# State space branch of a hybrid encoder: all products and sums on VectorE, in more and smaller steps, with earlier loads

## Chip, cores and metric

The kernel runs on one core of a Trainium2 chip. The metric is the device time of one execution in microseconds (us), median of several runs. PE is TensorE, DVE is VectorE, ACT is ScalarE, POOL is GpSimd, and SP is SyncE, whose queue issues most DMAs.

## What is computed

One layer of a trunk over 1024 positions of width 1024, in fp32: a norm, one input projection, three branches (a 2-D Fourier mix, a neighbourhood attention of 8 heads, a bidirectional state space scan), gates, an output projection, and a feed-forward part. The branch that the change touches is, cut down:

```python
def _ssm_scan(ug, a_re, a_im, log_dt, b_re, b_im, c_re, c_im, reverse):
    lam_bar = exp(lam * dt)                                # complex, 16 groups x 64 states
    b_bar = ((lam_bar - 1) / lam) * b
    bu = einsum('bsgc,gpc->bsgp', ug, b_bar)
    xs = associative_scan(x[s] = lam_bar * x[s-1] + bu[s]) # along the 1024 positions
    return real(einsum('bsgp,gcp->bsgc', xs, c))

y = d_skip * u + scan(forward) + scan(reverse)
y = gelu(y);  y = y * sigmoid(y @ w_glu)
```

## The kernel before

Every fp32 matrix is split into a high and a low part, and a product is three matmuls of 128x512 (L171, L165). Weights come through a queue (`w_next`, `w_cut`): a DMA, a cast on ACT (L142), a subtraction on DVE (L143). The program is written as one main stream on PE, in the order of a list of steps: the projection of the scan's input, eight tiles of v, then logits of the gates, the q and k projections of four pairs of heads, the gates and the rest. Two generators run beside it. `mm_main` calls `tick` after every third matmul; the state space branch (`ssm`) goes on by 0.4 steps at each tick, the attention by 0.57, where one step is the code up to the next `yield`. A scheduler then orders each engine's instructions by this program order and the buffers that are free; SBUF buffers come from pools (`m`: 21 buffers, `s`: 36), and PSUM has 8 banks (`ps`).

The state space branch works on four quarters q of 4 groups each. `ssm_params` computes the small coefficients, on POOL for the most part, among them `bbar` (POOL) and `bhat` (DVE). `ssm_prep` (generator `matrices`) makes for each quarter two matrices AA and BB by complex products (`product`, tiles of 128x512), the padded `bz`, the transposes BT of BB (PE L464, evicted by ACT L465), and a matrix M by way of `kp` (PE L469, ACT L473 to L475, DVE L477 and L478, eight small DMAs). `ssm_data` multiplies the input U with BT on PE, turns the result by E (L505 to L511), runs four scans (L515, L517), turns back (L523 to L530), and on PE multiplies with M and AA into Y, which is stored to `y_scr`. `ssm_gelu` loads two quarters as `yT` (L552) and applies the gelu on ACT and DVE (L555 to L561); at the end of `ssm` the weights `w_glu` are loaded, and the gate is computed (L597 to L626) and spilled to DRAM (`b_scr`), from where the gate step `u0` loads it as `act`.

In a complex product POOL and DVE share the six instructions of 128x512: POOL makes the two products L430 and L434 and the sum L437, DVE L431, L432 and L435. In `ssm_data` POOL makes `rz` (L495), two sums (L507, L511), two products and a sum of the turn back (L523, L527, L530).

Of the kernel before, what the change touches and what calls it, by code (L numbers as in the profile page):

```python
# [10 lines left out]
F32 = mybir.dt.float32  # L11
# [53 lines left out]
class Trunk:  # L65
# [354 lines left out]
    def ssm_prep(self, q):  # L420

        nc, V, G, A = self.nc, self.nc.vector, self.nc.gpsimd, self.nc.scalar
        g0 = 4 * q
        gs = slice(g0, g0 + 4)
        pa, bbar, bhat = self.ssm_pa, self.ssm_bb, self.ssm_bh

        def product(out, x, y, sh):

            t, u = self.m(sh, F32, "pt"), self.m(sh, F32, "pt")
            G.tensor_tensor(out=t, in0=x[1], in1=y[1], op=ALU.mult)  # L430
            V.tensor_tensor(out=out[:, 0], in0=x[0], in1=y[0], op=ALU.mult)  # L431
            V.tensor_tensor(out=u, in0=x[1], in1=y[0], op=ALU.mult)  # L432
            yield
            G.tensor_tensor(out=out[:, 1], in0=x[0], in1=y[-1], op=ALU.mult)  # L434
            V.tensor_tensor(out=out[:, 0], in0=out[:, 0], in1=t, op=ALU.subtract)  # L435
            yield
            G.tensor_tensor(out=out[:, 1], in0=out[:, 1], in1=u, op=ALU.subtract if len(y) == 3 else ALU.add)  # L437
            yield

        U = self.m([P, 4, NK], F32, "U")  # L440
        self.dma(U, self.u_scr[64 * q:64 * q + 64].rearrange("(g c) (s k) -> (c s) g k", g=4, k=NK))
        AA = self.s([P, 2, 4, 8, 16], F32, "AA")
        sh = [P, 4, 8, 16]
        yield from product(AA, [self.ssm_cc[:, i, gs, :].unsqueeze(2).to_broadcast(sh) for i in range(2)],
                           [pa[:, i, gs, :].unsqueeze(3).to_broadcast(sh) for i in range(3)], sh)
        BB = self.s([P, 2, 4, 16, 8], F32, "BB")
        sh = [P, 4, 16, 8]
        yield from product(BB, [bhat[:, i, gs, :].unsqueeze(3).to_broadcast(sh) for i in range(2)],
                           [pa[:, i, gs, ::-1].unsqueeze(2).to_broadcast(sh) for i in range(2)], sh)
        AA = AA.rearrange("p i g s c -> p i g (s c)")  # L450
        bz = self.m([P, 2, 4, 64], F32, "bz")
        G.memset(bz, 0.0)
        for i in range(2):
            G.tensor_copy(bz[0:64, i, :, 0:16], bbar[0:64, i, gs, :])
            G.tensor_copy(bz[64:128, i, :, 32:48], bbar[64:128, i, gs, :])
        yield
        for _ in range(5 if q == 0 else 0):
            yield
        BT = self.s([P, 4, 2, P], F32, "BT")
        for b in range(2):  # L460
            ps = self.ps([P, 2, 2, P])
            for j in range(2):
                for i in range(2):
                    nc.tensor.transpose(ps[:, j, i, :], BB[:, i, 2 * b + j].rearrange("p c s -> p (c s)"), self.ident)  # L464
            A.copy(BT[:, 2 * b:2 * b + 2], ps)  # L465
            yield
        ps = self.ps([64, 4, P])
        for j in range(4):
            self.mm(ps[:, j, :], [(bz[:, i, j, :], AA[:, i, j, :]) for i in range(2)])  # L469
        kp = self.s([16, 4, 15, 16], F32, "kp")  # L470
        psv = ps.rearrange("p g (s c) -> p g s c", s=8)
        kt = self.m([16, 4, 16], F32, "kt")
        A.copy(kp[:, :, 7:15, :], psv[0:16])  # L473
        A.copy(kp[:, :, 0:7, :], psv[32:48, :, 0:7, :])
        A.copy(kt, psv[32:48, :, 7, :])  # L475
        yield
        V.tensor_tensor(out=kt, in0=kt, in1=self.ssm_dd[:, gs, :], op=ALU.add)  # L477
        V.tensor_tensor(out=kp[:, :, 7, :], in0=kp[:, :, 7, :], in1=kt, op=ALU.add)  # L478
        yield
        M = self.m([P, 4, P], F32, "M")  # L480
        for s in range(8):
            self.dma(M[s::8], kp[:, :, 7 - s:15 - s, :].rearrange("p g t c -> p g (t c)"))
        yield
        self.ssm_mat[q] = (AA, BT, M, U)

    def ssm_data(self, q):
# [5 lines left out]
        L = 4 * NK  # L492
        flat = lambda t: t.rearrange("p g k -> p (g k)")
        rz = self.m(sh, F32, "rz")
        G.tensor_tensor(out=rz, in0=self.ssm_keep[:, 0, 4 * q:4 * q + 4].unsqueeze(2).to_broadcast(sh),  # L495
                        in1=self.kmask.unsqueeze(1).to_broadcast(sh), op=ALU.mult)
        pv = []
        for i in range(2):
# [5 lines left out]
        ta, tb, tc_, td = (self.m(sh, F32, "v") for _ in range(4))  # L504
        V.tensor_tensor(out=ta, in0=pv[0], in1=E[:, 0], op=ALU.mult)  # L505
        V.tensor_tensor(out=tb, in0=pv[1], in1=E[:, 1], op=ALU.mult)
        G.tensor_tensor(out=ta, in0=ta, in1=tb, op=ALU.add)  # L507
        yield
        V.tensor_tensor(out=tc_, in0=pv[1], in1=E[:, 0], op=ALU.mult)
        V.tensor_tensor(out=td, in0=pv[0], in1=E[:, 1], op=ALU.mult)  # L510
        G.tensor_tensor(out=tc_, in0=tc_, in1=td, op=ALU.subtract)  # L511
        yield
        zs = [self.m(sh, F32, "z") for _ in range(2)]
        for v, z in ((ta, zs[0]), (tc_, zs[1])):
            V.tensor_tensor_scan(out=flat(z)[0:64, 1:L], data0=flat(rz)[0:64, 0:L - 1], data1=flat(v)[0:64, 0:L - 1],  # L515
                                 initial=0.0, op0=ALU.mult, op1=ALU.add)
            V.tensor_tensor_scan(out=flat(z)[64:128, 0:L - 1][:, ::-1], data0=flat(rz)[64:128, 1:L][:, ::-1],  # L517
                                 data1=flat(v)[64:128, 1:L][:, ::-1], initial=0.0, op0=ALU.mult, op1=ALU.add)
            V.memset(z[0:64, :, 0], 0.0)
            V.memset(z[64:128, :, NK - 1], 0.0)  # L520
            yield
        ta, tb, tc_, td = (self.m(sh, F32, "v") for _ in range(4))
        G.tensor_tensor(out=ta, in0=zs[0], in1=E[:, 0], op=ALU.mult)  # L523
        V.tensor_tensor(out=tb, in0=zs[1], in1=E[:, 1], op=ALU.mult)
        V.tensor_tensor(out=td, in0=zs[1], in1=E[:, 0], op=ALU.mult)
        yield
        G.tensor_tensor(out=tc_, in0=zs[0], in1=E[:, 1], op=ALU.mult)  # L527
        V.tensor_tensor(out=ta, in0=ta, in1=tb, op=ALU.subtract)
        yield
        G.tensor_tensor(out=tc_, in0=tc_, in1=td, op=ALU.add)  # L530
        yield
        yield
        ps = self.ps(sh)
# [11 lines left out]
    def ssm_gelu(self, hf):  # L545
# [4 lines left out]
        for _ in range(3):  # L550
            yield
        self.tc.keep_in_program_order(self.dma(yT, self.y_scr[8 * hf:8 * hf + 8].rearrange("g c s k -> (g c) s k")))  # L552
        t1, g2 = self.s([P, 8, NK], F32, "t1"), self.s([P, 8, NK], F32, "g2")
        yield
        A.activation(t1, yT, AF.Square)  # L555
# [9 lines left out]
    def ssm(self):  # L565
# [9 lines left out]
        def data():  # L575
            for q in range(4):
                while q not in self.ssm_mat:
                    yield
                yield from self.ssm_data(q)

        def after():
            for hf in range(2):
                while self.y_done < 2 * hf + 2:
                    yield
                yield from self.ssm_gelu(hf)

        self.y_done = 0
# [1025 lines left out]
```

## Time and profile before

| | us |
|---|---|
| median of 3 runs | 1432.58 |
| lowest, highest | 1430.61, 1438.53 |
| the profiled execution | 1433.98 |
| its span | 1432.2 |
| PE busy in the span | 1383.5 |
| DVE, ACT, POOL busy | 947.0, 572.0, 188.8 |

Time zero is the start of the span. In a timeline a row has start, duration, engine, line, operation, tiles, shapes, and in brackets how long the engine idled before it and what ended that. In the table of stretches a row has the stretch, its length, the busy time of each engine with its instructions, the granted clock of PE as a share of 2.4 GHz (0.50 is the lower level, 1.2 GHz), the share of the DMA engines and GB/s. Matmuls overlap in the pipeline: a matmul of 128x512 lasts 0.39 us in a row, but rows follow each other every 0.227 us. On DVE rows overlap too, a little.

### The profile page before, as it was taken

Reading aid. Unit: us, or ns where it says so; the run is one execution under the profiler, and the core shown is the slowest. Engines: PE = TensorE matmul, PEld = TensorE weight load, DVE = VectorE, ACT = ScalarE, POOL = GpSimd, SP = SyncE. Lnnn points to the kernel's source line nnn. Section 1 sums busy time; section 2 is a strip of 40 time slices with the busy share of each in tenths; the row PEclk is TensorE's granted clock in tenths of the full one; section 3 lists DMA queues with packets and bytes.
Section 4 is the critical chain, followed back from the end, with each engine's and each line's share of the span. In section 5 each row is a group of like instructions: output and inputs, shape, how many; then the busy total and the mean of one; then the engine's idle time right before and its main releaser. Section 6 shows DMA issues by size and latency. Waiting matters only on the chain.

```text
span 1432.2 us, 18648 instructions
## 1 busy us (share of the span) xinstructions
PE 1383.5 (97%) x6520; PEld 1152.1 (80%) x6520; DVE 947.0 (66%) x1764; ACT 572.0 (40%) x1087; POOL 188.8 (13%) x313
## 2 busy tenths in 40 slices
PE   6999988999999999999999999999999999999997
PEld 5778877788888888888788878888888788888885
DVE  6759876576473312543524797777777999878766
ACT  5512264566562211032401674333323364444244
POOL 3758611000000000000000003112211100000000
PEclk9999999999999999999999999999999999999998
DMA  6332453737563217411343226444447885454303
GB/s 227 136 121 82 132 165 99 215 111 239 170 215 127 99 42 255 145 43 35 96 162 114 78 89 213 140 154 148 143 155 265 278 298 176 147 175 143 96 8 117
DMA packets 110926, 209.62 MB, mean 146 GB/s; under 512 B 13681, under 2 KB 46833, under 8 KB 110833
## 3 DMA queue, kind: packets, MB, share of 16 engines
q1 hardware_dynamic: 100160, 174.09, 37.6%
q0 software_dynamic: 10672, 34.35, 6.5%
q8 instruction: 51, 0.84, 0.2%
q14 instruction: 43, 0.34, 0.1%
HBM read 146.52 MB, written 56.62 MB: 142 GB/s over the span
## 4 chain that ended last, share of the span: by engine, by line
PE 83%; DVE 7%; DMA 2%; issue 2%; ACT 1%; POOL 1%; SPq 1%; DVEq 0%; ACTq 0%; POOLq 0%
PE ps L165 45%; PE ps L171 34%; PE ps L789 1%; PE ps L806 1%; PE ps L810 1%; SPq L111 1%; DVE z L515 1%; DVE z L517 1%; DVE wl L143 0%; DMA vj<-v_scr 0%; PE ps L1083 0%; DMA bm<-in_rpb 0%; DVE BB L431 0%; DMA wr<-in_w_in 0%; DVE sm L764 0%
## 5 line engine op out<-in xcount | busy, mean ns | idle before, releaser
L165 PE MATMUL ps<-dw,dh 128*128 128x512 f32 x1344 | 306.1, 389 | 2.3 <-DVE dw L197 2.3
L165 PE MATMUL ps<-fb,uw 128*128 128x512 f32 x1344 | 306.6, 389 | 1.4 <-DVE t L1142 1.0
L165 PEld LDWEIGHTS ps<-dw,dh 128*128 128x128 f32 x1344 | 252.0, 188 | 55.7 <-DVE dw L197 3.2
L165 PEld LDWEIGHTS ps<-fb,uw 128*128 128x128 f32 x1344 | 251.9, 188 | 54.5 <-PE ps L1083 1.2
L171 PE MATMUL ps<-hTh,wh 128*128 128x512 f32 x576 | 231.7, 403 | 6.3 <-DVE mx L764 2.0
L171 PE MATMUL ps<-hTl,wh 128*128 128x512 f32 x576 | 227.6, 395 | 1.1 <-DVE hTl L200 1.1
L171 PE MATMUL ps<-hTh,wl 128*128 128x512 f32 x576 | 226.9, 394 | 0.0
L171 PEld LDWEIGHTS ps<-hTh,wh 128*128 128x128 f32 x576 | 109.3, 190 | 28.0 <-ACT wh L142 2.4
L171 PEld LDWEIGHTS ps<-hTh,wl 128*128 128x128 f32 x576 | 109.0, 189 | 22.9
L171 PEld LDWEIGHTS ps<-hTl,wh 128*128 128x128 f32 x576 | 109.5, 190 | 21.2 <-DVE hTl L200 1.5
L143 DVE TENSOR_TENSOR wl<-wr,wh 128x1024 fp32r<-128x1024 f32 (+2 forms) x76 | 72.5, 966 | 55.3 <-ACT wh L142 52.3
L196 ACT CAST dh<-da 128x512 fp32r<-128x512 f32 x112 | 69.5, 620 | 95.4 <-PE ps L165 61.2
L1379 DVE TENSOR_TENSOR x<-x,ps 128x512 f32<-128x512 f32 x112 | 73.6, 684 | 34.4 <-PE ps L165 34.3
L1295 POOL DMA_DIRECT2D h_scr<-hx x48 | 26.0, 541 | 493.7 <-ACT hx L1265 376.1
L197 DVE TENSOR_TENSOR dh<-da,dh 128x512 fp32r<-128x512 f32 x112 | 77.1, 688 | 13.8 <-ACT dh L196 13.8
L171 PE MATMUL ps<-act,wh 128*128 128x512 f32 x256 | 78.7, 390 | 0.1
L142 ACT CAST wh<-wr 128x1024 fp32r<-128x1024 f32 (+2 forms) x76 | 60.7, 821 | 32.1 <-PE ps L171 7.7
L196 ACT CAST uw<-us 128x512 fp32r<-128x512 f32 x64 | 38.1, 626 | 84.2 <-DVE us L1222 84.2
L1017 ACT ACTIVATE tg<-ps 128x512 f32<-128x512 f32 x32 | 19.1, 597 | 124.0 <-PE ps L171 118.6
L1267 DVE SCALAR_TENSOR_TENSOR hx<-hx 128x512 f32<-128x512 f32 x52 | 35.8, 689 | 40.7 <-ACT hx L1259 40.3
L764 DVE CUSTOM_DVE_ANT_0 sm<-ps,bm 128x384 f32<-128x384 f32 x64 | 35.3, 553 | 34.2 <-PE ps L165 24.2
L196 ACT CAST dw<-wd 128x512 fp32r<-128x512 f32 x80 | 49.4, 618 | 19.1 <-PE ps L165 18.4
(286 smaller groups left out, 2116.6 us busy)
## 6 DMA issues: line engine op xcount, KB each, us to landing
da<-h_scr SPq DMA_DIRECT2D x112, 256.0 KB
wr<-in_w_in SPq DMA_DIRECT2D x36, 512.0 KB
wu<-in_w_up SPq DMA_DIRECT2D x32, 512.0 KB
h_scr<-hs POOLq DMA_DIRECT2D x64, 256.0 KB, 2.6
wd<-in_w_down SPq DMA_DIRECT2D x64, 256.0 KB
bm<-in_rpb SPq DMA_DIRECT2D x64, 192.0 KB
h_scr<-hx POOLq DMA_DIRECT2D x48, 256.0 KB, 2.8
vj<-v_scr SPq DMA_DIRECT2D x128, 64.0 KB
```

Of the source, the lines that this page charges most:

```text
L111: return self.nc.sync.dma_start(out=out, in_=in_)
L142: self.nc.scalar.copy(hi, r)
L143: self.nc.vector.tensor_tensor(out=lo, in0=r, in1=hi.bitcast(F32), op=ALU.subtract)
L165: self.nc.tensor.matmul(out=out, lhsT=l, rhs=r, start=start and i == 0, stop=stop and i == last, skip_group_check=more)
L171: self.nc.tensor.matmul(out=out, lhsT=l, rhs=r, start=i == 0, stop=i == last)
L196: nc.scalar.copy(hi, src)
L197: nc.vector.tensor_tensor(out=lo, in0=src, in1=hi.bitcast(F32), op=ALU.subtract)
L764: V.tensor_tensor_reduce(out=sm, in0=ps[:, 0:384], in1=bm.pop(u), scale=-1.0, scalar=3.0e38, op0=ALU.add, op1=ALU.min, accum_out=mx)
L1017: A.activation(tg, ps, AF.Tanh, scale=0.5)
L1267: V.scalar_tensor_tensor(out=x, in0=x, scalar=0.0, in1=x, op0=ALU.max, op1=ALU.mult)
L1295: self.nc.gpsimd.dma_start(out=self.t.h_scr[c, j - 1], in_=x)
L1379: self.nc.vector.tensor_tensor(out=self.x1[t][:, cs], in0=self.x1[t][:, cs], in1=self.banks[j][q], op=ALU.add)
```

## The change

DVE does what POOL did in the products and in `ssm_data`; ACT does POOL's copies into `bz` (only its memset stays on POOL). `product` uses one temporary instead of two, and the turn back writes into the tiles of the turn before. There are more `yield`s: one more in the turn, two more in the scans, one more for the first quarter before BT, and six more between the load of `yT` and its use. The load of `w_glu` stands ahead of the second half's gelu.

```diff
         def product(out, x, y, sh):
-            t, u = self.m(sh, F32, "pt"), self.m(sh, F32, "pt")
-            G.tensor_tensor(out=t, in0=x[1], in1=y[1], op=ALU.mult)
+            t = self.m(sh, F32, "pt")
+            V.tensor_tensor(out=t, in0=x[1], in1=y[1], op=ALU.mult)
             V.tensor_tensor(out=out[:, 0], in0=x[0], in1=y[0], op=ALU.mult)
-            V.tensor_tensor(out=u, in0=x[1], in1=y[0], op=ALU.mult)
             yield
-            G.tensor_tensor(out=out[:, 1], in0=x[0], in1=y[-1], op=ALU.mult)
             V.tensor_tensor(out=out[:, 0], in0=out[:, 0], in1=t, op=ALU.subtract)
+            V.tensor_tensor(out=t, in0=x[1], in1=y[0], op=ALU.mult)
             yield
-            G.tensor_tensor(out=out[:, 1], in0=out[:, 1], in1=u, op=ALU.subtract if len(y) == 3 else ALU.add)
+            V.tensor_tensor(out=out[:, 1], in0=x[0], in1=y[-1], op=ALU.mult)
+            V.tensor_tensor(out=out[:, 1], in0=out[:, 1], in1=t, op=ALU.subtract if len(y) == 3 else ALU.add)
             yield
...
         for i in range(2):
-            G.tensor_copy(bz[0:64, i, :, 0:16], bbar[0:64, i, gs, :])
-            G.tensor_copy(bz[64:128, i, :, 32:48], bbar[64:128, i, gs, :])
-        yield
-        for _ in range(5 if q == 0 else 0):
+            A.copy(bz[0:64, i, :, 0:16], bbar[0:64, i, gs, :])
+            A.copy(bz[64:128, i, :, 32:48], bbar[64:128, i, gs, :])
+        yield
+        for _ in range(6 if q == 0 else 0):
             yield
...
-        G.tensor_tensor(out=rz, ...)
+        V.tensor_tensor(out=rz, ...)
...
         V.tensor_tensor(out=tb, in0=pv[1], in1=E[:, 1], op=ALU.mult)
-        G.tensor_tensor(out=ta, in0=ta, in1=tb, op=ALU.add)
         yield
         V.tensor_tensor(out=tc_, in0=pv[1], in1=E[:, 0], op=ALU.mult)
         V.tensor_tensor(out=td, in0=pv[0], in1=E[:, 1], op=ALU.mult)
-        G.tensor_tensor(out=tc_, in0=tc_, in1=td, op=ALU.subtract)
+        yield
+        V.tensor_tensor(out=ta, in0=ta, in1=tb, op=ALU.add)
+        V.tensor_tensor(out=tc_, in0=tc_, in1=td, op=ALU.subtract)
         yield
...
+            V.memset(z[0:64, :, 0], 0.0)
+            yield
             V.tensor_tensor_scan(out=flat(z)[64:128, 0:L - 1][:, ::-1], ...)
-            V.memset(z[0:64, :, 0], 0.0)
             V.memset(z[64:128, :, NK - 1], 0.0)
             yield
-        ta, tb, tc_, td = (self.m(sh, F32, "v") for _ in range(4))
-        G.tensor_tensor(out=ta, in0=zs[0], in1=E[:, 0], op=ALU.mult)
+        V.tensor_tensor(out=ta, in0=zs[0], in1=E[:, 0], op=ALU.mult)
         V.tensor_tensor(out=tb, in0=zs[1], in1=E[:, 1], op=ALU.mult)
+        yield
         V.tensor_tensor(out=td, in0=zs[1], in1=E[:, 0], op=ALU.mult)
-        yield
-        G.tensor_tensor(out=tc_, in0=zs[0], in1=E[:, 1], op=ALU.mult)
+        V.tensor_tensor(out=tc_, in0=zs[0], in1=E[:, 1], op=ALU.mult)
+        yield
         V.tensor_tensor(out=ta, in0=ta, in1=tb, op=ALU.subtract)
-        yield
-        G.tensor_tensor(out=tc_, in0=tc_, in1=td, op=ALU.add)
+        V.tensor_tensor(out=tc_, in0=tc_, in1=td, op=ALU.add)
         yield
...
         self.tc.keep_in_program_order(self.dma(yT, ...))      # ssm_gelu
+        for _ in range(6):
+            yield
...
                 while self.y_done < 2 * hf + 2:               # ssm, after()
                     yield
+                if hf == 1:
+                    glw.append(self.m([P, 2, 2, P], F32, "glw"))
+                    self.dma(glw[0], self.a["w_glu"])
                 yield from self.ssm_gelu(hf)
...
-        wr = self.m([P, 2, 2, P], F32, "glw")
-        self.dma(wr, self.a["w_glu"])
-        self.split(wh, wl, wr)
+        self.split(wh, wl, glw.pop())
```

The scheduler gives every engine another order of instructions from the first quarter's matrices on; from the fourth pair of heads to the end the orders are the same. Line numbers of the changed kernel lie up to 6 above those of before. Numbers behind a tile's name tell its instances apart.

DVE at the first quarter's matrices, before, from the first product of BB to its real part (vt is the low part of a tile of v, bhat the coefficients of which BB is made, pt the temporaries):

```order
L431 TENSOR_TENSOR BB_819<-bhat_751,pa_746 128x512
L244 TENSOR_TENSOR bhat_751<-tb_759 128x256
L435 TENSOR_TENSOR AA_784<-AA_784,pt_785 128x512
L197 TENSOR_TENSOR vt_811<-ps_775,vt_811 128x8x64
L432 TENSOR_TENSOR pt_821<-bhat_751,pa_746 128x512
L435 TENSOR_TENSOR BB_819<-BB_819,pt_820 128x512
```

DVE at the same place, now:

```order
L431 TENSOR_TENSOR BB_818<-bhat_751,pa_746 128x512
L436 TENSOR_TENSOR BB_818<-bhat_751,pa_746 128x512
L433 TENSOR_TENSOR AA_784<-AA_784,pt_785 128x512
L197 TENSOR_TENSOR vt_810<-ps_775,vt_810 128x8x64
L244 TENSOR_TENSOR bhat_751<-tb_759 128x256
L434 TENSOR_TENSOR pt_785<-ssc_507,pa_746 128x512
L430 TENSOR_TENSOR pt_819<-bhat_751,pa_746 128x512
L437 TENSOR_TENSOR AA_784<-AA_784,pt_785 128x512
L433 TENSOR_TENSOR BB_818<-BB_818,pt_819 128x512
L197 TENSOR_TENSOR vt_847<-ps_814,vt_847 128x8x64
L434 TENSOR_TENSOR pt_819<-bhat_751,pa_746 128x512
L437 TENSOR_TENSOR BB_818<-BB_818,pt_819 128x512
```

From AA's first product to BB's last sum DVE now has 20 instructions, 14 of 512 and 6 of 256 columns, where it had 13, 7 and 6; PE has six more matmuls of the main stream ahead of the first transposes of BB.

ACT at the start of the first pair of heads, before (t is the gelu's tile, BT the transposes of the last quarter's BB, kp a part of its M, sm the scores, tg a gate's logits):

```order
L1042 ACTIVATE tg_1642<-ps_1572 128x512
L555 ACTIVATE t_287_1620<-yT_1535 128x1024
L465 COPY BT_1659<-ps_1660 128x512
L465 COPY BT_1659<-ps_1675 128x512
L559 ACTIVATE t_287_1620<-t_287_1620 128x1024
L473 COPY kp_1701<-ps_1692 16x4x128
```

ACT at the same place, now:

```order
L465 COPY BT_1612<-ps_1613 128x512
L142 CAST wh_1673<-wr_1504 128x1024
L465 COPY BT_1612<-ps_1633 128x512
L777 ACTIVATE sm_1643,su_1646<-sm_1643,mx_1644 128x384
L1048 ACTIVATE tg_1668<-ps_1574 128x512
L777 ACTIVATE sm_1656,su_1659<-sm_1656,mx_1657 128x384
```

The gelu of the first half (L555, now L558) stands 47 instructions behind the second eviction of BT, at the end of this pair; in SP's queue the load of `yT` for it stands right behind the eight DMAs of the last quarter's M, which start from `kp`.

DVE between the first and the second pair of heads, before (OT is the attention's output, spl its low part; L764 reads the second pair's first scores):

```order
L819 TENSOR_TENSOR OT_1584<-ps_2361,ot_2396 64x16x16
L819 TENSOR_TENSOR OT_1584<-ps_2373,ot_2409 64x16x16
L197 TENSOR_TENSOR spl_2424<-OT_1584,sph_2423 128x1024
L143 TENSOR_TENSOR wl_2475<-wr_2341,wh_2474 128x1024
L764 ISA sm_2512,mx_2513<-ps_2509,bm_2444 128x384
```

DVE at the same place, now, up to the scans (L505 and L506 stand just ahead):

```order
L825 TENSOR_TENSOR OT_1523<-ps_2299,ot_2331 64x16x16
L825 TENSOR_TENSOR OT_1523<-ps_2311,ot_2346 64x16x16
L511 TENSOR_TENSOR v_2340<-v_2340,v_2341 128x512
L508 TENSOR_TENSOR v_2342<-ps_2323,E_638 128x512
L509 TENSOR_TENSOR v_2343<-ps_2294,E_638 128x512
L197 TENSOR_TENSOR spl_2362<-OT_1523,sph_2361 128x1024
L512 TENSOR_TENSOR v_2342<-v_2342,v_2343 128x512
L143 TENSOR_TENSOR wl_2419<-wr_2275,wh_2418 128x1024
L516 SCALAR_TENSOR_TENSOR z_2398<-rz_2292,v_2340 64x511
L520 SCALAR_TENSOR_TENSOR z_2398<-rz_2292,v_2340 64x511
L516 SCALAR_TENSOR_TENSOR z_2399<-rz_2292,v_2342 64x511
L520 SCALAR_TENSOR_TENSOR z_2399<-rz_2292,v_2342 64x511
```

The last quarter's data steps (20 instructions on DVE, four of them scans, ten behind the rows shown) now stand here, ahead of the second pair's first scores (now L770). Before they stood among the first pair's scores, where the third quarter's now stand. From the first pair's first scores to the second pair's DVE has 18 more instructions of 128x512, four more scans and four more small memsets than before. The 24 matmuls of the gate (L597 to L626) with their work on ACT and DVE have moved from the second pair of heads to the third.

## Rows read from the trace of the kernel before

**Rows 1.** The page's part 1: busy time, share of the span, instructions.

```profile
PE 1383.5 (97%) x6520; PEld 1152.1 (80%) x6520; DVE 947.0 (66%) x1764; ACT 572.0 (40%) x1087; POOL 188.8 (13%) x313
```

**Rows 2.** Stretches: length, busy PE, PEld, DVE, ACT, POOL, clock, DMA, GB/s.

```profile
79.90:83.10 3.20, 0.39 (x3) 0.20 (x2) 3.16 (x4) 0.00 (x0) 3.20 (x5) 0.88 0.40 164
83.10:89.20 6.10, 6.10 (x18) 5.02 (x19) 0.69 (x1) 1.66 (x3) 2.47 (x6) 0.50 0.64 258
89.20:174.70 85.50, 85.17 (x459) 70.96 (x457) 70.40 (x83) 21.68 (x36) 61.28 (x49) 1.00 0.35 100
174.70:242.00 67.30, 55.94 (x321) 47.82 (x321) 47.59 (x110) 36.82 (x82) 9.18 (x7) 0.95 0.46 132
242.00:255.70 13.70, 13.70 (x62) 11.33 (x61) 3.29 (x4) 4.40 (x7) 0.00 (x0) 1.00 0.67 222
255.70:324.00 68.30, 63.95 (x329) 53.49 (x328) 47.16 (x104) 43.81 (x91) 0.00 (x0) 0.98 0.54 162
324.00:410.00 86.00, 86.00 (x464) 74.03 (x463) 51.95 (x145) 52.23 (x121) 0.00 (x0) 1.00 0.66 195
```

**Rows 3.** PE's timeline, single rows from 79 to 277 us.

```profile
79.31 0.39 PE L171 MATMUL ps<-wl,hTh 128*128 128x512 f32 x1
79.54 0.39 PE L171 MATMUL ps<-wh,hTl 128*128 128x512 f32 x1
...
82.01 0.30 PE L464 MATMUL ps<-konst,BB 128*128 128x128 f32 x1 [2.08 <-DVE BB L435]
...
181.58 0.49 PE L165 MATMUL ps<-U,M 128*128 128x128 f32 x2 [1.96 <-ACT BT L465]
...
188.90 0.52 PE L789 MATMUL ps<-konst,sm 128*128 128x128 f32 x3 [2.23 <-DVE sm L781]
...
276.54 0.62 PE L789 MATMUL ps<-konst,sm 128*128 128x128 f32 x3 [2.31 <-ACT sm L779]
```

**Rows 4.** DVE's timeline, the first quarter's matrices.

```profile
69.63 0.68 DVE L431 TENSOR_TENSOR AA<-ssc,pa 128x512 f32<-128x512 f32 x1
...
78.22 0.41 DVE L244 TENSOR_TENSOR bhat<-tb 128x256 f32<-128x256 f32 x1
78.56 0.68 DVE L435 TENSOR_TENSOR AA<-AA,pt 128x512 f32<-128x512 f32 x1
79.16 0.68 DVE L197 TENSOR_TENSOR vt<-ps,vt 128x512 fp32r<-128x512 f32 x1
```

**Rows 5.** POOL's timeline, a step of the coefficients.

```profile
63.13 0.65 POOL L240 TENSOR_TENSOR tb<-ssb,pt 128x256 f32<-128x256 f32 x1
```

**Rows 6.** DVE by form, 40 to 340 us: busy, mean ns, idle before.

```profile
L517 DVE TENSOR_TENSOR_SCAN z<-rz,v 64x511 f32<-64x511 f32 x8 | 12.5, 1564 | 0.2
...
L431 DVE TENSOR_TENSOR BB<-bhat,pa 128x512 f32<-128x512 f32 x4 | 5.6, 1401 | 0.0
...
L623 DVE SCALAR_TENSOR_TENSOR y<-tg,g 128x512 f32<-128x512 f32 x4 | 4.6, 1159 | 0.1
```

**Rows 7.** DVE's timeline: a scan beside busy POOL, and one without it.

```profile
136.58 2.13 DVE L517 TENSOR_TENSOR_SCAN z<-rz,v 64x511 f32<-64x511 f32 x1
...
217.72 1.22 DVE L517 TENSOR_TENSOR_SCAN z<-rz,v 64x511 f32<-64x511 f32 x1
```

**Rows 8.** ACT's timeline: both halves' gelu, with the idle time before.

```profile
180.00 1.06 ACT L555 ACTIVATE t<-yT 128x1024 f32<-128x1024 f32 x1 [12.08 <-DMA wr<-in_w_in]
...
259.68 1.06 ACT L555 ACTIVATE t<-yT 128x1024 f32<-128x1024 f32 x1 [3.28 <-DMA yT<-y_scr]
```

**Rows 9.** SP's timeline: when the first half's load is issued.

```profile
174.49 0.43 SPq L111 DMA_DIRECT2D yT<-y_scr  x1
```

**Rows 10.** Waits of DVE, 174.7 to 255.7 us: total, times, longest.

```profile
DVE OT L819 <- ACT ot L818: 7.3, 2, 7.1
DVE t L557 <- ACT t L555: 5.7, 1, 5.7
```

**Rows 11.** Issues of the loads of b_scr: ns, first and last start.

```profile
L111 SPq DMA_DIRECT2D act<-b_scr x24: 319/380/679, 414.7 to 579.4; - x24
```

More of the change, by code (lines that the diff above doesn't have):

```diff
@@ L494, in ssm_data @@
         rz = self.m(sh, F32, "rz")
-        G.tensor_tensor(out=rz, in0=self.ssm_keep[:, 0, 4 * q:4 * q + 4].unsqueeze(2).to_broadcast(sh),
+        V.tensor_tensor(out=rz, in0=self.ssm_keep[:, 0, 4 * q:4 * q + 4].unsqueeze(2).to_broadcast(sh),
                         in1=self.kmask.unsqueeze(1).to_broadcast(sh), op=ALU.mult)
@@ L579, in data @@
                 yield from self.ssm_data(q)
+        glw = []
         def after():
```

## The prediction

> **What bounds the kernel now.** I read the page's busy times first, then the table of stretches, then the waits of the engine that bounds. PE is busy for 1383.5 of the span's 1432.2 us [rows 1]: it is the bound nearly everywhere, so the change can only pay where PE idles or runs at the lower clock, and only lose where it makes PE wait. The stretches show where the state space branch makes PE do either [rows 2]. From 89.20 to 174.70 us PE has no gap (85.17 of 85.50), although DVE is busy for 70.4 and POOL for 61.3 there. Three places lose time. The first is the first quarter's matrices: 79.90 to 83.10 has 0.39 us of PE, and the 6.10 us behind it run at half the clock. The second is the first pair of heads (174.70 to 255.70, two rows, 81.0 us): 67.30 − 55.94 = 11.36 us idle and a clock of 0.95. The third is the second pair: 68.30 − 63.95 = 4.35 us idle and 0.98. The third pair (324.00 to 410.00) loses nothing. What ended the idle times [rows 3]: a part of BB from DVE (2.08 us), BT from ACT (1.96), sm from DVE (2.23) and from ACT (2.31).
>
> **First quarter's matrices.** PE now loses 3.20 − 0.39 = 2.81 us idle, and 6.10 us at half clock give back 3.05 us less work [rows 2]: 5.86 us. In the changed kernel DVE makes everything alone: 14 instructions of 512 and 6 of 256 columns from AA's first product, which started at 69.63. In a row they follow each other at 0.60 us (78.56 to 79.16) and 0.34 us (78.22 to 78.56) [rows 4]; so BB is ready at 69.63 + 14 × 0.60 + 6 × 0.34 + 0.2 for the last one's end = 80.3. Before, it was ready only at about 82.0, since DVE's instructions beside POOL were long: the products L431 of BB lasted 1.40 us on average [rows 6]. PE would reach the transposes at 82.01 − 2.08 = 79.93, and has six more matmuls of the main stream ahead of them, at 0.227 us each (79.31 to 79.54 in the rows, rounded) [rows 3]: 81.3. The unknown is POOL: its last four coefficient instructions (L241 to L244), now scattered among products, come right behind L240, four at 0.65 us [rows 5], 2.6 us in which DVE's small steps ahead of 69.63 may stretch. I take 1.5 us of that, the middle and a little: BB at 81.8, 0.5 to 0.7 us of idle time, and no half clock, since the half clock came behind a gap of 2.8. **Gain 5.2 us.** Bounds: 5.9 (no gap at all), and 1.1 (the whole 2.6, so 1.7 idle, and the half clock stays).
>
> The rows show what running beside POOL costs: the same scan took 2.13 us at 136.58, while POOL worked, and 1.22 us at 217.72 without it [rows 7]. The Trainium skill gives a reason ("SBUF — State Buffer", Who interferes with whom): DVE and GpSimd share a port pair as an exclusive lock, so the one that loses waits for the other's whole instruction. By that rule the whole 2.6 us would be lost, and this gain would lie between 1.1 and 4.2 us. The trace agrees that something is shared, but a stretch from 1.22 to 2.13 is less than POOL's time, so I keep the middle.
>
> **From 89.20 to 174.70.** DVE gets 28 products of 128x512 more there and gives four with a PSUM input and four scans to later: 24 × 0.60 − 4 × 1.22 [rows 4, 7] = +9.5 us on 70.4, 79.9 of 85.5 [rows 2], even if no instruction becomes shorter now that POOL is idle; and some will, as the scans do (mean 1.56 against 1.22 us [rows 6, 7]). I cost it at nothing; PE's matmuls cover it. If that cover is thin at one place, up to 2 us.
>
> **First pair of heads.** ACT waited 12.08 us for `yT` ahead of its gelu at 180.00 [rows 8], since the load was issued at 174.49 only [rows 9]. Behind the gelu on ACT stood both evictions of BT; so PE waited 1.96 us for BT, and later 2.23 for sm, which DVE had begun late, having waited 5.7 us for the gelu itself [rows 3, 10]. Now BT's evictions stand 47 instructions ahead of the gelu: these 4.2 us go. Against it stands DVE. It was busy for 47.59 + 3.29 = 50.9 us of the 81.0 [rows 2], and gets 18 × 0.60 + 4 × 1.22 = 15.7 more: 66.6. PE without idle time and clock loss needs 81.0 − 11.36 − 0.05 × 67.3 = 66.2. The two are level, so what counts is how much of DVE's 30.1 us of waits stays. Three blocks should go: 5.7 for the gelu, 7.1 for `ot` [rows 10], since DVE is no longer ahead of PE there, and the 13.70 − 3.29 = 10.4 at the end [rows 2], where the last quarter's data steps now stand. With those gone 6.9 us stay: 73.5. From PE's side, if all but the 4.2 stays, 76.8. I take 75, between them: **gain 6.0 us**. Bounds: 14.8 (66.2, no loss left) and a loss of 2.9 (the last block finds no free time: 66.6 + 17.3 = 83.9).
>
> What is late next is the second pair's start: the last quarter's 20 instructions (12 × 0.60 + 4 × 1.22 = 12.1 us) come on top of 3.29 in 13.70 us, 1.7 too many; a late DVE holds PE at the first sm. I take half, 0.8.
>
> **Second and third pair.** In the second, the gate leaves. ACT's wait of 3.28 us for the second `yT` at 259.68 [rows 8] and PE's 2.31 us at 276.54 [rows 3] with the clock loss behind it, 0.02 × 68.3 = 1.4 [rows 2], go: −2.3 − 1.4 + 0.8 = **gain 2.9 us**. Bounds: 5.8 (4.35 + 1.4, no loss left) and a loss of 1.7 (the stalls stay, DVE is late in full). The third pair gets the gate and the gelu's second half: four instructions of 1.16 us (L623) [rows 6] and two of 1.2 or so on DVE, 7 us on 51.95 of 86.0 [rows 2]. There is room, but the gate's chain through ACT and DVE made gaps where it stood. **Loss 1.2 us**, half of 2.31; bounds nothing and 3.7 (2.3 + 1.4). The gate's later stores must land ahead of the loads of `b_scr`, the first issued at 414.7 [rows 11]; the gate stands inside the third pair, which ends at 410.0, so this costs nothing. From the fourth pair on nothing changes.
>
> **Sum**, against the profiled execution's 1433.98 us: −5.2 − 6.0 − 2.9 + 1.2 = −12.9, so 1421 us. That execution lies 1.4 above the median of 1432.58 and inside the runs' spread (1430.61 to 1438.53); I don't take the 1.4 off.
>
> **Rivals.** (1) *Nothing is left over:* with free engines the three places lose nothing: −5.9 − 14.8 − 5.8 = −26.5, 1407.5 us. For it: PE's third pair runs so today with DVE at 60%. Against: DVE's 66.6 in the first pair would have to fit without a gap. (2) *A wait is replaced by a wait:* POOL's bunched steps stretch DVE's chain, the first BB is late as before (−1.1), and in the first pair PE waits for DVE's sm as long as it did for BT (0); −1.1 − 2.9 + 1.2 = −2.8, 1431 us. For it: the two engines are level there. (3) *DVE becomes the bound of the first pair, and the program slower:* if DVE keeps its 30.1 us of waits, which the attention's chain through PE, ACT and DVE causes and not the work's amount, the stage lasts 66.6 + 30.1 = 96.7, +15.7; with the first gain kept and nothing from the second pair, −5.2 + 15.7 + 1.2 = +11.7, 1445.7 us. It decides from 81.0 − 66.6 + 5.2 − 1.2 = 18.4 us of DVE waits in that stage. Against it: over 20 of the 30.1 lie where DVE had run out of work. The Trainium skill speaks for this rival ("Perfetto Trace Analysis", Optimizing Scalar/DVE Operations): if DVE is saturated, it advises giving work away, to GPSIMD too, while it warns that moves between these two may not help because they share a port. The change goes the other way; the trace agrees with the warning at the scans, and says of saturation only that DVE is near it in this one stage.
>
> **Chances.** The forecast (1414 to 1427) 0.57, rival 1 0.10, rival 2 0.24, rival 3 0.09. Within 0.5% (7.2 us, about what a measurement of this kernel can tell from no change) means 1425.4 to 1439.7. Faster: rival 1 and nearly all of the forecast's, 0.62; the same: its upper end, rival 2 and the lower part of rival 3, 0.31; slower: 0.07. The range of 8 in 10: down to 1410, where most of rival 1 is left out, and up to 1434, which takes in rival 2 and leaves out rival 3.
>
> **What will show it.** First BB: PE's row of the first L464 transposes should have a wait under 1 us, and the stretch behind it clock 1.00; a wait of 2 says that POOL's steps stretched the chain. First pair: no wait of ACT for `yT` ahead of BT, DVE busy for 64 to 67 us in 73 to 77; if DVE is under 80% busy and the stage is longer than 81, rival 3 holds. Second pair: PE idle under 3 us. Third: PE idle of 1 us or so. Scans at 1.22 us throughout. The prediction falls if PE gets a gap between 89 and 174 us, which I cost at nothing, or if one of the first pair's gaps drops PE to half clock for long.

## The result, and the profile after

The changed kernel took 1418.05 us (median of 4 runs, 1417.74 to 1419.28) against 1432.65 of the kernel before in the same comparison: a ratio of 0.9893, 95% interval 0.9864 to 0.9923, so 14.6 us or 1.1% less. Forecast were 1421 us and a gain of 12.9. The profiled execution took 1417.89 us, its span 1416.1.

Part 1 of the page of the changed kernel:

```profile
PE 1378.0 (97%) x6520; PEld 1150.0 (81%) x6520; DVE 952.3 (67%) x1812; ACT 577.3 (41%) x1103; POOL 109.2 (8%) x249
```

Against [rows 1] PE idles 38.1 us instead of 48.7 and is busy for 5.5 us less with as many matmuls; 2.8 us of that, summed over stretches of 2 us, are less time lost at the lower clock. DVE, with 48 instructions more, is busy for only 5.3 us more.

Stretches of the changed kernel (columns as in [rows 2]): the way to the first transposes of BB, what follows, the way to the first scores, the first, the second and the third pair of heads:

```profile
63.73:83.00 19.27, 19.27 (x86) 15.94 (x86) 19.05 (x53) 5.86 (x13) 4.87 (x8) 1.00 0.29 108
83.00:95.00 12.00, 12.00 (x65) 9.82 (x64) 3.45 (x7) 2.96 (x6) 0.00 (x0) 1.00 0.42 162
95.00:168.34 73.34, 73.34 (x393) 61.32 (x392) 61.62 (x96) 24.51 (x46) 1.05 (x2) 1.00 0.37 108
168.34:242.02 73.68, 68.29 (x374) 58.74 (x373) 58.73 (x133) 39.22 (x86) 0.00 (x0) 0.93 0.56 163
242.02:303.40 61.38, 61.38 (x343) 53.10 (x342) 44.45 (x103) 41.70 (x87) 0.00 (x0) 1.00 0.61 178
303.40:370.00 66.60, 64.81 (x344) 55.07 (x343) 42.88 (x99) 40.11 (x86) 0.00 (x0) 1.00 0.60 178
```

The first place of loss is empty in this profile; e10 below shows that a gap of 0.97 us belongs there. In the first pair 73.68 − 68.29 = 5.39 us of idle time stay, at a mean clock of 0.93; the second pair has no gap; the third, where the gate now is, has 1.79 us. PE's waits in these stretches, from its timeline:

```profile
188.49 0.74 PE L812 MATMUL ps<-p,vj 128*128 128x256 f32 x4 [0.86 <-DVE p L197]
192.83 1.01 PE L165 MATMUL ps<-qk,qk 128*128 128x384 f32 x2 [3.21 <-DVE z L518]
198.19 0.90 PE L795 MATMUL ps<-konst,sm 128*128 128x128 f32 x3 [1.32 <-DVE sm L787]
...
341.24 0.52 PE L795 MATMUL ps<-konst,sm 128*128 128x128 f32 x3 [0.22 <-DVE p L197]
344.66 0.39 PE L812 MATMUL ps<-p,vj 128*128 128x256 f32 x1 [1.57 <-ACT p L196]
```

Of the waits of [rows 3] those for BB and BT are gone; one for sm from DVE is still there, 1.32 us now, behind the longest wait. That one, 3.21 us, is new, and DVE's timeline tells how it comes about:

```profile
187.88 0.56 DVE L197 TENSOR_TENSOR p<-ps,p 128x384 fp32r<-128x384 f32 x1 [4.80 <-ACT p L196]
...
188.42 1.20 DVE L516 TENSOR_TENSOR_SCAN z<-rz,v 64x511 f32<-64x511 f32 x1
189.65 1.22 DVE L520 TENSOR_TENSOR_SCAN z<-rz,v 64x511 f32<-64x511 f32 x1
190.90 1.28 DVE L729 SCALAR_TENSOR_TENSOR qk<-ps,qk 64x512 fp32r<-64x512 f32 x2
...
192.72 0.06 DVE L518 MEMSET z<- 64x4 f32 x1
```

These rows follow the order of DVE's program. DVE stood idle for 4.80 us ahead of L197, which makes the low part of p (the attention's weights, turned by PE) and waited for ACT's high part. Two scans stood behind it. When it was done the scans took 2.4 us, and only then came the low parts of the projection (L729, into `qk`) and the next score. PE's wait ended at 192.83, behind the memset L518, which follows these in DVE's queue.

### The profile page after: what moved, and what is told of

It is laid out like the page before. It is cut to its first block, busy times and chain, and to the rows that moved or that the text cites. A ratio compares the mean times of both kernels' runs of the same rounds, so it can differ in the third digit from the quotient of the medians.

```text
span 1416.1 us, 18593 instructions
## 1 busy us (share of the span) xinstructions
PE 1378.0 (97%) x6520; PEld 1150.0 (81%) x6520; DVE 952.3 (67%) x1812; ACT 577.3 (41%) x1103; POOL 109.2 (8%) x249
## 3 DMA queue, kind: packets, MB, share of 16 engines
q1 hardware_dynamic: 100160, 174.09, 38.1%
## 4 chain that ended last, share of the span: by engine, by line
PE 94%; DVE 3%; ACT 1%; issue 1%; DMA 1%; POOL 0%; SPq 0%; POOLq 0%; ACTq 0%
PE ps L165 47%; PE ps L171 43%; PE ps L795 1%; PE ps L812 1%; PE ps L816 1%; DMA x<-in_x 1%; PE ps L1089 0%; ACT hTh L199 0%; DVE t L1335 0%; ACT wh L142 0%; PE ps L464 0%; ACT h L219 0%; DVE x L221 0%; DVE x L1385 0%; DVE wd L1335 0%
## 5 line engine op out<-in xcount | busy, mean ns | idle before, releaser
L143 DVE TENSOR_TENSOR wl<-wr,wh 128x1024 fp32r<-128x1024 f32 (+2 forms) x76 | 70.7, 941 | 59.8 <-ACT wh L142 57.0
L196 ACT CAST dh<-da 128x512 fp32r<-128x512 f32 x112 | 69.4, 620 | 98.2 <-PE ps L165 61.3
L197 DVE TENSOR_TENSOR dh<-da,dh 128x512 fp32r<-128x512 f32 x112 | 77.5, 692 | 16.1 <-ACT dh L196 16.0
L142 ACT CAST wh<-wr 128x1024 fp32r<-128x1024 f32 (+2 forms) x76 | 60.8, 821 | 32.9 <-DMA wr<-in_w_br_fn 13.2
L196 ACT CAST uw<-us 128x512 fp32r<-128x512 f32 x64 | 38.1, 625 | 84.2 <-DVE us L1228 84.2
L171 PEld LDWEIGHTS ps<-act,wh 128*128 128x128 f32 x256 | 47.7, 188 | 10.0 <-ACT wh L142 0.5
```

Of the source, the lines that this page charges most:

```text
L142: self.nc.scalar.copy(hi, r)
L143: self.nc.vector.tensor_tensor(out=lo, in0=r, in1=hi.bitcast(F32), op=ALU.subtract)
L171: self.nc.tensor.matmul(out=out, lhsT=l, rhs=r, start=i == 0, stop=i == last)
L196: nc.scalar.copy(hi, src)
L197: nc.vector.tensor_tensor(out=lo, in0=src, in1=hi.bitcast(F32), op=ALU.subtract)
```

## Experiments

The waits of PE at four places in each kernel's profile, summed from its timeline (us; without the time lost at the lower clock), and the medians:

| kernel | first BB | first pair | second | third | median us |
|---|---|---|---|---|---|
| before | 2.81 | 11.35 | 4.12 | 0 | 1432.65 |
| changed | 0 | 5.39 | 0 | 1.79 | 1418.05 |
| e1, engines without the loads | 0.97 | 8.90 | 0 | 0 | 1419.09 |
| e2, loads without the engines | 2.78 | 5.22 | 0 | 0 | 1418.27 |
| e3, POOL in the products | 1.43 | 5.94 | 0 | 1.79 | 1420.14 |
| e4, changed, POOL kept busy | 3.71 | 5.94 | 0 | 1.79 | 1439.31 |
| e5, scans earlier | 0.98 | 2.08 | 0 | 0 | 1411.70 |
| e6, scans in pairs | 0.97 | 6.86 | 0 | 0 | 1417.07 |
| e7, both | 0 | 8.71 | 0 | 0 | 1421.49 |
| e8, bbar on DVE | 0 | 4.53 | 0 | 1.79 | 1416.41 |
| e9, scans earlier, bbar on DVE | 0 | 2.66 | 0 | 0 | 1410.48 |
| e10, changed, again | 0.97 | 6.17 | 0 | 1.78 | 1418.79 |

The kernel before had medians from 1432.65 to 1433.95 us in the four comparisons. The 2.81 us at its first BB are the 2.08 of [rows 3] and a wait right behind it:

```profile
83.04 0.90 PE L464 MATMUL ps<-konst,BB 128*128 128x128 f32 x3 [0.73 <-POOL BB L437]
```

The changed kernel, e7 and e9 were profiled in executions in which PE came late to this place (a clock of 0.84 to 0.86 from 30 to 40 us, where the kernel before, e1 to e3, e5, e6, e8 and e10 have 1.00), so of the zeros in the first column only e8's tells something of the kernel. e4 waits for 9.05 us more at places between the first two columns.

**e1, the engines without the earlier loads.** From the changed kernel:

```diff
         self.tc.keep_in_program_order(self.dma(yT, ...))
-        for _ in range(6):
-            yield
...
-                if hf == 1:
-                    glw.append(self.m([P, 2, 2, P], F32, "glw"))
-                    self.dma(glw[0], self.a["w_glu"])
...
+        wr = self.m([P, 2, 2, P], F32, "glw")
+        self.dma(wr, self.a["w_glu"])
...
-        self.split(wh, wl, glw.pop())
+        self.split(wh, wl, wr)
```

> The changed kernel without its earlier loads: no steps between the load of yT and the gelu, and the load of w_glu behind the gelu again. Theory A (the prediction's: the earlier loads are worth the 4.2 us at the first pair of heads and most of the second pair's gain of 2.3 + 1.4): about 6 to 8 us slower than the changed kernel's 1418.05, 1424 to 1426 us, with a wait of ACT for yT of 2 us or more in front of a gelu and PE waiting for BT or sm. Theory B (the longer engine program of DVE has already moved the gelu behind the last quarter's BT, so the loads add nothing): 1417 to 1420 us, and no PE wait for BT.

Ratio to before 0.9901 (0.9888 to 0.9915). Theory B held in its number and in its reason. ACT's timeline of e1 has the last eviction of BT far ahead of the gelu, without the six steps:

```profile
167.92 0.59 ACT L465 COPY BT<-ps 128x512 f32<-128x512 f32 x1 [1.70 <-PE ps L464]
...
192.12 1.06 ACT L556 ACTIVATE t<-yT 128x1024 f32<-128x1024 f32 x1
```

So the rest of the change had moved the last quarter's matrices and the gelu apart by itself. Whether DVE's longer program or the added steps in it did so was not tested. The loads still do something: with them the waits of the first pair are 5.39 us (6.17 in e10) and not 8.90, but 1.79 come in the third pair. The medians do not show it.

**e2, the loads without the engines.** The same edit the other way round, put into the kernel before.

> The kernel before with the earlier loads alone (six steps between the load of yT and its use, w_glu loaded ahead of the second gelu); POOL keeps its products. Theory A: the stalls of 1.96 and 2.23 us at the first pair and the 2.31 us plus lower clock of the second pair go, the gap at the first quarter's BB (2.81 us and 3.05 us of half clock) stays: 1432.65 - 4.2 - 2 to 3 = 1425 to 1427 us. Theory B (the gain hangs on the engines, and another stall takes the place): 1430 us or more. BB's gap stays under both: a PE wait near 2 us ahead of the first transposes.

Ratio 0.9895 (0.9879 to 0.9910). Neither theory: the loads alone brought the whole gain, 7 us more than A gave them. PE's timeline of e2:

```profile
81.89 0.30 PE L464 MATMUL ps<-konst,BB 128*128 128x128 f32 x1 [2.05 <-DVE BB L435]
82.93 0.55 PE L464 MATMUL ps<-konst,BB 128*128 128x128 f32 x3 [0.73 <-POOL BB L437]
...
198.55 0.62 PE L165 MATMUL ps<-qk,qk 128*128 128x384 f32 x2 [1.02 <-DVE mx L769]
200.75 0.51 PE L171 MATMUL ps<-hTh,wh 128*128 128x512 f32 x1 [1.12 <-DVE v L509]
213.55 0.79 PE L171 MATMUL ps<-hTh,wh 128*128 128x512 f32 x1 [2.04 <-DVE mx L769]
225.34 0.55 PE L794 MATMUL ps<-konst,sm 128*128 128x128 f32 x3 [1.04 <-ACT sm L784]
```

and ACT's at the last quarter's BT:

```profile
169.48 0.59 ACT L465 COPY BT<-ps 128x512 f32<-128x512 f32 x1 [1.19 <-PE ps L464]
...
177.76 1.06 ACT L557 ACTIVATE t<-yT 128x1024 f32<-128x1024 f32 x1 [0.33 <-DMA yT<-y_scr]
```

BB's gap is untouched, as both theories had it; the clock from 83 to 90 us is 0.76 (0.56 before). ACT now evicts BT 8 us ahead of the gelu, so the 1.96 and 2.23 us of [rows 3] are gone, as forecast; beyond the forecast the second pair lost all its 4.12 us of waits, and the gate, now at its end (290 to 308 us), makes no gap.

**e3, POOL back in the products of the matrices.** `product` as before, all else as changed.

> The changed kernel with the complex products of the matrices (AA, BB) shared between POOL and DVE as before; the rest as changed. Theory A (the first gain comes from DVE working alone): the gap ahead of the first transposes of BB is back, 2 us or so with half clock behind it, 4 to 6 us slower than the changed kernel: 1422 to 1424 us. Rival (the six more matmuls ahead of the transposes, not the engines, close the gap): gap under 1 us there, 1417 to 1420 us.

Ratio 0.9906 (0.9893 to 0.9920), 1420.14 us (1416.87 to 1421.06): nearer to the rival. PE's timeline of e3 at the first BB:

```profile
82.28 0.30 PE L464 MATMUL ps<-konst,BB 128*128 128x128 f32 x1 [0.69 <-DVE BB L435]
83.32 0.55 PE L464 MATMUL ps<-konst,BB 128*128 128x128 f32 x3 [0.74 <-POOL BB L437]
```

The gap is 0.69 + 0.74 us, and the clock from 83 to 90 us is 1.00. BB's real part comes 17.5 us behind POOL's step L240 here as in the kernel before (63.39 to 80.89, 63.13 to 80.64), so the products have gained nothing. The six more matmuls (6 × 0.227 = 1.4 us) close half of the 2.81 us without any change of engine in the products, and the half clock goes with it; DVE alone takes off about half a microsecond more (0.97 in e1 and e10).

**e4, the changed kernel with POOL kept busy.** Six products of 128x512 on POOL in `ssm_prep` and six in `ssm_data`, for each quarter:

```diff
+        self.dummy(6, U, pa[...])
         yield from product(AA, ...)
...
         V.tensor_tensor(out=rz, ...)
+        self.dummy(6, rz, rz)
```

> The changed kernel with 48 POOL instructions of 128x512 added, six at each quarter's matrices and six at each quarter's data, whose results nobody reads; nothing waits for them, and the order on PE, DVE and ACT is that of the changed kernel. So the cost of running beside POOL stands alone. Theory A (that cost is what the first gap was made of): scans beside POOL near 1.5 us on average instead of 1.22, the chain of the first BB 2 to 4 us longer, a PE gap of 1 to 3 us there with half clock behind it: 1421 to 1425 us. Rival (DVE has room everywhere, the gain came from the order alone): longer DVE instructions, but no PE gap, 1417 to 1420 us.

Ratio 1.0048 (1.0035 to 1.0061): slower than the kernel before, and 21 us slower than the changed one, far above theory A's 3 to 7. The direction was right, the size not, since I looked at the first quarter alone. DVE's and ACT's instructions stand in the order of the changed kernel. DVE's groups of e4 (by form, 60 to 340 us):

```profile
L521 DVE TENSOR_TENSOR v<-v,v 128x512 f32<-128x512 f32 x4 | 4.9, 1216 | 0.1
...
L516 DVE TENSOR_TENSOR v<-ps,E 128x512 f32<-128x512 f32 x4 | 2.7, 683 | 0.0
```

The sum L521 (L511 of the changed kernel, 0.69 us there) took 1.22 on average, while the product with an operand in PSUM (L516) stayed at 0.68. PE's timeline shows where it hurts, at the matrices of the first, the second and the fourth quarter (the third's pass without a gap):

```profile
86.01 0.44 PE L466 MATMUL ps<-konst,BB 128*128 128x128 f32 x1 [2.31 <-DVE BB L434]
...
126.12 1.55 PE L165 MATMUL ps<-AA,bz 128*64 128x128 f32 x10 [3.28 <-DVE z L532]
129.39 1.54 PE L466 MATMUL ps<-konst,BB 128*128 128x128 f32 x6 [1.72 <-DVE BB L438]
183.54 0.55 PE L466 MATMUL ps<-konst,BB 128*128 128x128 f32 x3 [3.07 <-DVE BB L438]
```

The 3.28 us that the trace puts down to a memset are AA's: its last sum (L438) ended at 125.97, just ahead of it in DVE's queue. PE idles 1437.3 − 1386.0 = 51.3 us here, 13.2 more than in the changed kernel, and is busy 8.0 more at the lower clock: together the 21.2 us of the spans. With all products on DVE, three of the four quarters' matrices had no room for this beside POOL.

**e5, the scans one step earlier.** To try the reading of the 3.21 us:

```diff
         V.tensor_tensor(out=td, in0=pv[0], in1=E[:, 1], op=ALU.mult)
-        yield
         V.tensor_tensor(out=ta, in0=ta, in1=tb, op=ALU.add)
```

> The changed kernel without the added step between the products of the turn and its sums, so that a quarter's scans come one step earlier; in the first pair of heads the first two scans then stand ahead of the products p (L197) instead of behind them. Theory A (PE's 3.21 us wait in the first pair comes from DVE's queue: 4.80 us idle for ACT's p, with two scans of 1.2 us right behind it and the eviction of k behind these): no wait of 3 us there, the 1.32 us behind it and the half clock go too, 6 to 9 us gained: 1409 to 1412 us. Rival (DVE's amount of work in that pair is the limit, the scans then delay sm or OT instead): gaps of the same sum at other places of the pair, 1416 to 1420 us.

Ratio 0.9844 (0.9828 to 0.9860), 1411.70 us: theory A. DVE's timeline of e5:

```profile
179.26 1.20 DVE L515 TENSOR_TENSOR_SCAN z<-rz,v 64x511 f32<-64x511 f32 x1
180.49 1.22 DVE L519 TENSOR_TENSOR_SCAN z<-rz,v 64x511 f32<-64x511 f32 x1
...
181.86 0.56 DVE L197 TENSOR_TENSOR p<-ps,p 128x384 fp32r<-128x384 f32 x1
...
189.98 0.68 DVE L728 SCALAR_TENSOR_TENSOR qk<-ps,qk 64x512 fp32r<-64x512 f32 x1 [1.02 <-ACT qk L727]
```

The scans now stand ahead of p, and the first eviction of the projection waits for ACT and no longer for them. Of the first pair's waits 2.08 us stay, the longest 1.55. The trace puts this one down to the load of a bias tile, but ACT's sm (L784, 190.45 to 191.05) ended just before PE went on at 191.10, and in e9 the same wait, 1.51, is put down to ACT's sm. The third pair's 1.79 are gone as well, which was not expected.

**e6, both scans of a tensor in one step.**

```diff
             V.memset(z[0:64, :, 0], 0.0)
-            yield
             V.tensor_tensor_scan(out=flat(z)[64:128, ...)
```

> The changed kernel with both scans of a tensor in one step, as before the change; two steps fewer per quarter, and the scans leave the p products of the first pair ahead of them. Theory A as above: the 3.21 us wait goes, 1409 to 1412 us. Rival: each pair of scans holds DVE for 2.4 us in one piece, so PE waits for sm by 1 to 2 us in two or three places: 1416 to 1421 us.

Ratio 0.9881 (0.9864 to 0.9897), 1417.07 us. The 3.21 us wait went, but the rival's number came true: other waits took its place, the two longest in PE's timeline of e6:

```profile
195.14 0.67 PE L794 MATMUL ps<-konst,sm 128*128 128x128 f32 x3 [1.95 <-ACT sm L784]
...
224.17 0.90 PE L794 MATMUL ps<-konst,sm 128*128 128x128 f32 x3 [2.67 <-ACT sm L784]
```

**e7, both edits.** Three steps fewer per quarter.

> Both of these edits in one: three steps fewer per quarter, so the state space branch ends its last quarters earlier. Theory A: the third quarter's scans are over before the first scores, no wait of 3 us in the first pair, and the last quarter's data fall into the pair's end; 1409 to 1413 us. Rival (DVE bound in the first pair): two or three gaps of 1 to 2 us in the first pair as in the kernel before, 1416 to 1420 us.

Ratio 0.9913 (0.9899 to 0.9927), 1421.49 us (1421.31 to 1423.36): the rival's side, a little above its range, though only two scans are left in the pair's first part (168.16 and 169.41). The gelu and the last quarter's data now come in the pair's middle (on DVE from 193.9 and 200.3 us on), and PE waits seven times, five of them for DVE; the two longest:

```profile
196.47 0.55 PE L793 MATMUL ps<-konst,sm 128*128 128x128 f32 x3 [2.15 <-DVE p L197]
...
212.48 0.47 PE L171 MATMUL ps<-hTh,wh 128*128 128x512 f32 x1 [2.02 <-DVE p L197]
```

So one step fewer is better, two (e6) change nothing that can be measured, and three are worse. I read this as the place of DVE's long instructions among the pair's short ones, and not the number of steps; which of them costs e7 its waits was not tested.

**e8, bbar on DVE.** The six instructions of `bbar` leave POOL; DVE makes them, placed in the program behind BB's products. The scheduler has put two steps of bhat ahead of the first AA in return.

> The changed kernel with the six instructions of bbar (128x256) on DVE, behind the first products, so that POOL does nothing beside DVE's small steps ahead of the first AA. In the changed kernel the way from POOL's first tb step to DVE's first product of AA took 8.43 us, before 6.50. Theory A (the stretch is POOL's four bunched steps): 5.5 to 6.5 us now, but six instructions of 0.34 us more on DVE, most of them among the products: BB's transposes 0 to 1 us earlier, total 1417 to 1419 us (same). Rival (the stretch is DVE's own order): 8 us or more, BB 2 us later, a PE gap of 2 us or more.

Ratio 0.9882 (0.9866 to 0.9897), 1416.41 us. Theory A. DVE in the changed kernel, from its first step behind the coefficients to the first AA and the end of BB:

```profile
63.23 0.58 DVE L239 TENSOR_TENSOR pt<-pt 128x16 f32<-128x16 f32 x1 [6.25 <-POOL pt L244]
...
64.85 0.71 DVE L241 TENSOR_TENSOR pt<-pt 128x16 f32<-128x16 f32 x1
...
72.16 0.68 DVE L431 TENSOR_TENSOR AA<-ssc,pa 128x512 f32<-128x512 f32 x1
...
82.24 0.69 DVE L437 TENSOR_TENSOR BB<-BB,pt 128x512 f32<-128x512 f32 x1
```

and in e8:

```profile
62.71 0.17 DVE L239 TENSOR_TENSOR pt<-pt 128x16 f32<-128x16 f32 x1 [6.27 <-POOL pt L244]
...
63.48 0.17 DVE L241 TENSOR_TENSOR pt<-pt 128x16 f32<-128x16 f32 x1
...
69.55 0.69 DVE L435 TENSOR_TENSOR AA<-ssc,pa 128x512 f32<-128x512 f32 x1
...
80.37 0.70 DVE L441 TENSOR_TENSOR BB<-BB,pt 128x512 f32<-128x512 f32 x1
```

8.93 us became 6.84, although the two steps of bhat now stand in between. The rows show where the time was: beside POOL's four steps L241 to L244 four of DVE's small steps took 0.71, 0.60, 0.59 and 0.71 us in the changed kernel, and 0.17 or 0.18 each in e8, 1.9 us less together. The first gap is gone, and here the clock was 1.00 from 30 us on to this place, so PE did not come late.

**e9, e5 and e8 in one kernel, and e10, the changed kernel once more.**

> The earlier scans (no step between the turn's products and sums) and bbar on DVE in one kernel. If the two gaps are independent, the 0.98 us at the first BB that the kernel with earlier scans still had goes too, and 1.7 us of gaps and some half clock in the first pair stay: 1411.7 less 1 to 2, 1409.5 to 1411 us. If the earlier arrival at the first pair moves its gaps: 1411 to 1415 us.

> The changed kernel once more, on the chip of the kernel above. Theory (in its first profile the gap ahead of the first BB was hidden only because PE was late, at a granted clock of 0.85 from 30 to 40 us): where the clock there is 1.00, a PE gap of 0.9 to 1.0 us ahead of the second transposes of BB, without half clock behind it; total 1417 to 1419 us. Rival: no gap there at full clock either. The 3.21 us wait in the first pair is there in any case.

On one chip e9 took 1410.48 us, ratio 0.9833 (0.9813 to 0.9854), e10 1418.79, ratio 0.9887 (0.9868 to 0.9907). So e9 beats both kernels by a clear margin; over e5, taken on another chip, the 1.2 us are within the spread. e9's expectation held in its number; that the gap at the first BB went by the edit its profile can't show, since PE came late there (above). e10's held in full. PE's timeline of e10 has the first gap that the changed kernel's first profile did not show:

```profile
82.59 0.55 PE L464 MATMUL ps<-konst,BB 128*128 128x128 f32 x3 [0.97 <-DVE BB L437]
...
192.53 1.01 PE L165 MATMUL ps<-qk,qk 128*128 128x384 f32 x2 [3.20 <-DVE z L518]
```

The stretch from 30 to 50 us, in the changed kernel's first profile:

```profile
30.00:50.00 20.00, 17.29 (x86) 14.07 (x84) 15.85 (x28) 14.08 (x21) 16.29 (x46) 0.91 0.19 58
```

and in e10:

```profile
30.00:50.00 20.00, 18.05 (x94) 14.78 (x93) 16.57 (x28) 15.04 (x21) 16.46 (x45) 1.00 0.21 61
```

With 86 matmuls instead of 94 PE came to the transposes later, which would hide the 0.97 us.

## Why the prediction was right, step by step

**First matrices: right, and its unknown too.** The gain was 2.81 + 3.05 − 0.97 = 4.9 us in e10, forecast 5.2 with a gap of 0.5 to 0.7; the 5.9 of the first profile are luck, since PE came late there. From POOL's step L240 (63.73 in the changed kernel, 63.13 in [rows 5]) to the first AA it is 72.16 − 63.73 = 8.43 us, against 69.63 − 63.13 = 6.50: the bunched steps cost 1.9 of the 2.6 us at stake, where I took 1.5, and e8 shows by taking them away that it was they. From AA to BB's end the timeline has 82.93 − 72.16 = 10.8, the sum had 10.6. One reading was wrong: the "about 82.0" of before is BB's real part; its last sum, on POOL, was ready only at 83.0 (the row of 83.04 above). And of the two reasons in the sum, BB earlier and PE later by six matmuls, the second does most: e3 has it alone, with POOL still at work, and keeps 2.81 − 1.43 + 3.05 = 4.4 of the 4.9 us.

**89 to 168: right.** No gap; DVE busy 61.6 of 73.3 us, 84%, where the sum allowed for 79.9 of 85.5. The changed kernel's groups of DVE (by form, 60 to 340 us) show what ended:

```profile
L520 DVE TENSOR_TENSOR_SCAN z<-rz,v 64x511 f32<-64x511 f32 x8 | 9.8, 1219 | 0.2
...
L431 DVE TENSOR_TENSOR BB<-bhat,pa 128x512 f32<-128x512 f32 x4 | 2.7, 686 | 0.0
```

1.22 us against 1.56, 0.69 against 1.40 in [rows 6].

**First pair: right in size, wrong in the path.** From the first scores to the second pair's first scores it took 73.68 us, forecast 75, before 80.8:

```profile
174.74:255.54 80.80, 69.44 (x380) 58.99 (x380) 50.84 (x114) 41.22 (x89) 9.18 (x7) 0.96 0.50 147
```

The stalls behind the gelu went as the step says: ACT's row of the gelu is at 214.29, with no wait, and BT stands far ahead. But the 75 was a middle between two ends, PE's other losses staying (76.8) and DVE as the bound (73.5), and neither is what happened, so that the size came out is in part luck. DVE was busy for 58.73 of 73.68 us, not 66.6. Up to DVE's own first score of the second pair (244.6) it is 61.3; the rest is for the most part what I had left out, one L143 fewer (1.2 us) and the instructions that became shorter once POOL was still (in this pair the turn's L525 from 1.21 to 0.69 us, sm's from 0.60 to 0.41). Of PE's other losses the waits of 2.37, 2.04, 1.14, 0.98 and 0.63 us went too, and new ones came: above all one in DVE's queue, 3.21 us, and the lower clock behind it. e5, which takes that away, is 6.4 us faster, 1.8 of these in the third pair. The trace of before had not this wait, so no row could have shown it; the order could have: the two scans stand there behind three p in a row. I looked at how much DVE has to do, not at what it would wait for with the scans behind it.

**Second pair: mis-sized.** Forecast 2.9, measured 4.12 us of waits and the 1.4 of the clock: all that the pair had to lose. The 0.8 for a late DVE did not come. **Third pair:** 1.79 lost, forecast 1.2; that it is no price of the gate as such is shown by e5, which has it at 299 to 327 us, at the start of the third pair, without a gap.

**What the sum hid.** It came out within 3 us, but its parts are not additive. I gave the engines 5.2 us and the loads the rest. Each alone is worth nearly all: 1432.65 to 1418.27 for the loads, to 1419.09 for the engines (with the added steps), 1418.05 for both. Both move the last quarter's BT and the gelu apart. Why the rest of the two gains overlaps too is less clear: the loads alone leave the gap at BB (2.78 us in e2) and have no scans behind p, the engines alone close the gap and bring the scans (3.21 us in e1), which may be an even trade. Which of the three scheduler orders is worth how much in each pair was not worked out instruction by instruction; that stays open.

**The rivals.** Rival 1 needed the first pair without a gap; e9 comes within 3 us of its 1407.5. Rival 2 is excluded in its number, with the first gap down to 0.97 us and the first pair's waits halved; but in kind it was there, since a wait of 3.21 us for DVE took the place of those for BT and sm. Rival 3 is excluded: it needed more than 81 us in the first pair with 18 us or more of DVE's waits, and the pair took 73.7 with DVE idle for 15. e7 shows how near it was: with a few steps moved, five waits for DVE in that pair, and 83.0 us (167.49 to 250.46).

## What to carry to other kernels

When an engine gets more work, read in its new order what stands in front of each long instruction and behind it. Here two scans behind an instruction that waited for another engine delayed all that followed by their 2.4 us, though the engine had been idle for 4.8 us just before. Where two parts of a change act through the same schedule, don't add their gains; run each alone. And a few steps more or less in an interleaved generator can be worth nearly half of the change itself (6 us less, 3 us more), so try its neighbours.

## What the runs showed of the hardware

POOL lengthens DVE's instructions on SBUF operands (0.69 to 1.22 us on average in e4) and leaves those with an operand in PSUM alone (0.68 in both); kept up over all quarters it cost 21 us of a kernel in which DVE is busy for two thirds. The Trainium skill ("SBUF — State Buffer", Who interferes with whom) calls the port pair that the two share an exclusive lock, which one of them holds for its whole instruction while the other is blocked. The trace agrees that an instruction with both inputs in SBUF is held up; that it waits for a whole instruction of POOL's no run here shows: at the first bunch four small steps of DVE grew by 0.4 to 0.5 us each beside POOL's steps of 0.65 to 1.07, 1.9 of the 2.6 us that the prediction would have lost by this rule.

PE's clock after a gap differs from run to run: behind 3.2 us in the first pair the ten microseconds from 190 had a granted clock of 0.53 in the first profile of the changed kernel and 0.66 in the second, and behind the 0.97 us at BB (e10) it stayed at 1.00.
